# Sixteen modulation units spread anew over the recurrence's tail, a down projection and attention

## The chip, the cores and the metric

The kernel runs on one NeuronCore of a Trainium2 chip. The core has a matrix engine (TensorE, PE in the profile, with its weight loads shown as PEld), a vector engine (DVE), a scalar engine (ACT), a general engine (POOL) and a queue engine (SP) that issues nearly all transfers. Each engine runs its own instructions in the order in which they stand in the program, and waits on semaphores where it needs another engine's result. The metric is the device time of one execution in microseconds (us); lower is better.

## The reference, cut to what matters

One inference step of a two-layer encoder: a layer of RWKV-7 time mixing, then one of chunk-band attention, each followed by a gated feed-forward layer. There are 1024 prompt tokens and 8 x 16 sample tokens of width 1024, so nine conditioning vectors `c`. The vectors enter through an adaptive norm in front of each sub-layer:

```python
mod = silu(c) @ w_ada[l] + b_ada[l]                 # per layer, 1024 -> 6 * 1024
sh_m, sc_m, gt_m, sh_f, sc_f, gt_f = split(mod, 6)
x = x + gt_m * mixer(rms_norm(x) * (1 + sc_m) + sh_m)
h = rms_norm(x) * (1 + sc_f) + sh_f
x = x + gt_f * ((silu(h @ w_gate[l]) * (h @ w_up[l])) @ w_down[l])
# between the layers, for the keys and values that attention shares:
shift, scale = split(silu(c) @ kv_ada_w + kv_ada_b, 2)
k, v = split((rms_norm(x) * (1 + scale) + shift) @ w_kv, 2)
```

Everything is float32. The modulation depends on `c` alone, so it can be computed at any time before it is used.

## The kernel before

All 14 x 1024 columns of modulation (six of each layer, two of the shared keys and values) are cut into 28 **units** of 512 columns. Unit `u` fills the four columns `4u` to `4u+3` of the tile `mod`, each of 128 features by nine vectors. Units 0 to 11 belong to the first layer. Of the second, units 12 to 15 are the shift and scale in front of attention, 16 and 17 its gate, and 18 to 23 the shift, scale and gate of the feed-forward layer. Units 24 to 27 are the shift and scale of the shared keys and values.

A unit is made by `ada_steps` (line 194), a generator that other loops advance with `self.step(n)` (line 189). It has four steps. Each loads 512 KB of weights (line 201) into a tile from `rawtile` (line 226) and multiplies them with `scT` (line 204), four matmuls that the compiler issues as eight instructions, into one PSUM bank. The fourth step also copies the bank to SBUF on ScalarE (line 208), sums and turns it by four more matmuls (line 210, again eight instructions), and adds the bias on VectorE into `mod` (line 214). Consumers rescale `mod` in `gain` (line 217) and read it in `normed`, `normed_split` and `residual`.

The kernel runs through these stages:

- **Projections and recurrence** (`layer0a`, line 1088). Tokens are cut into three blocks of 384. The projections of a block are woven by hand with the recurrence's windows of the block before (`alternate`, line 1004). Units 0 to 3 run at the start. `proj` (line 461) then makes a generator of units 4 to 11, of which the last block's `proj_v` takes eight steps. The **tail** (lines 1101 to 1113) holds the last six windows, in steps, woven five to two with `early` (line 1105). This takes the remaining steps of the units, then the output projection (`outproj`, line 1062) of the first two token blocks, eight weight units each. The third block follows after the windows (line 1115). In the tail `rawtile` has two buffers, which the units, their copies and the output projection's weights share.
- **The first feed-forward layer** (`ffn`, line 1267): gate and up projections in a form with seven products instead of eight, then the **down projection** (lines 1277 to 1327). It has eleven rounds `p` of two weight rows, each with two column ranges `c`; `begin(p)` (line 1282) loads a round and calls `self.step(7)`. Units 12 to 27 run here, with PSUM bank `acc` and tiles `h0`.
- **Shared keys and values, first queries** (`kv`, line 1428).
- **Attention** (`attention`, line 1496): eight head pairs (`pair`, line 1602), sixteen query tiles each. `advance` (line 1633) starts a new tile, moves the two tiles before it one stage on (scores, softmax, transpose, output) and takes two pieces from `self.qgen`, which projects the queries of a later pair in the PSUM bank `acc` (one buffer, `head_steps`, line 1402). `kprep` and `qprep` (lines 1479, 1489) load the next pair's keys and queries. Loads here come from `slot(1)` (line 1152), a ring `h1` of fourteen tiles that also holds the normalised inputs of the sample-side columns.
- **Output projection and the second feed-forward layer.**

What stands in the code is not the final order of an engine's instructions. A planner in the compiler takes the instructions by priority (their order in the code) as a model of the machine makes them ready, and gives out buffers as they come free. A step that waits for a buffer lets a later one pass on the matrix engine, if that one is ready.

Of the kernel before, what the change touches and what calls it, by code (L numbers as in the profile page):

```python
# [10 lines left out]
AF = mybir.ActivationFunctionType  # L11
ALU = mybir.AluOpType
# [52 lines left out]
PAR = {n: i * 8 for i, n in enumerate(PARS)}  # L65
# [71 lines left out]
def mm(nc, out, lhsT, rhs, start, stop):  # L137
    return nc.tensor.matmul(out, lhsT, rhs, start=start, stop=stop)  # L138


class Trunk:
# [52 lines left out]
    def ada_steps(self, units, tag="aux", bufs=1):  # L194

        nc = self.nc
        for u in units:
            ps = self.bank(tag, bufs)
            for i in range(4):
                w = self.rawtile()  # L200
                nc.sync.dma_start(w[:, :1024], self.a["wada"][u, i])
                c = slice(i // 2 * 256, i // 2 * 256 + 256)
                for q in range(4):
                    mm(nc, ps[32 * q:32 * q + 32, c], self.scT[:, i % 2 * 4 + q, :], w[:, q * 256:q * 256 + 256], i % 2 == 0, i % 2 == 1)
                if i < 3:
                    yield
            sb = self.rawtile()[:, :512]
            nc.scalar.activation(sb, ps, AF.Copy)
            for j in range(4):
                mm(nc, ps[:, j * 16:(j + 1) * 16], sb[:, j * 128:(j + 1) * 128], self.C("qs"), True, True)  # L210
            pv = ps[:, 0:64].rearrange("p (j n) -> p j n", n=16)[:, :, 0:9]
            bo = PAR["bada"] + u * 4
            bv = self.par[:, bo:bo + 4].rearrange("p (j o) -> p j o", o=1).broadcast_to([128, 4, 9])
            nc.vector.tensor_tensor(self.mod[:, u * 4:u * 4 + 4, :], pv, bv, ALU.add)
            yield

    def gain(self, name, sc):

# [242 lines left out]
    def proj(self, b):  # L461

        if b == 0:
            self.ada = self.ada_steps((0, 2, 1, 3), "acc", 2)
            self.A0 = [self.cp.tile([128, 9], F32, name=f"A0_{f}") for f in range(8)]
            self.proj_h(0)
            self.lora_weights()
            self.x = self.hsplit()
            self.ada = self.ada_steps(range(4, 12))
        x, k = self.x, self.mixed(2, b)  # L470
        yield from self.proj_lora(b, *x)
        r = self.mixed(0, b)
        yield from self.proj_k(b, *k)
        v = self.mixed(3, b)
        yield from self.alternate(self.inverses(b), self.proj_r(b, *r))
        if b + 1 < NB:
            self.proj_h(b + 1)
        yield from self.proj_v(b, *v)
        if b + 1 < NB:
            self.x = self.hsplit()  # L480
# [607 lines left out]
    def layer0a(self, ctx):  # L1088
        self.yg = [self.dp.tile([128, 8, TB], F32, name=f"yg{b}") for b in range(NB)]
        c1, cw, ct = ExitStack(), ExitStack(), ExitStack()  # L1090
        self.ps = c1.enter_context(self.tc.tile_pool(name="psA", bufs=1, space=PSUM, reuse_waits="tile"))
        self.win_open(cw)
        with ExitStack() as c2:
            self.proj_open(c2)
            for _ in self.proj(0):
                pass
            for b in range(1, NB):
                w = self.windows([(w, hf) for w in range(3 * b - 3, 3 * b) for hf in range(2)])
                for _ in self.alternate(w, self.proj(b), 5, 4):
                    pass  # L1100
        self.tail_open(ct)
        self.nraw, self.nhi, self.nlo = (2, 2, 2)
        self.nmix, self.nmr = 16, 2

        def early():
            for _ in range(32):
                if next(self.ada, StopIteration) is StopIteration:
                    break
                yield
            for b in range(2):  # L1110
                yield from self.outproj(b)
        for _ in self.alternate(self.windows([divmod(int(x), 2) for x in '12 13 16 14 15 17'.split()]), early(), 5, 2):
            pass
        cw.close()
        for _ in self.outproj(2):
            pass
        ct.push(c1)
        return ct.close
# [148 lines left out]
    def ffn(self, l, B, W, part1, xsrc, dst, done):  # L1267

        nc = self.nc
        sd = [self.dp.tile([128, 2, 1152], F32, name=f"sd{l}_{p}") for p in range(11)]  # L1270
        self.gate_up(sd[0][:, 0], B, iter(W), (0,))
        for _ in part1:
            pass
        self.gate_up(sd[0][:, 0], B, iter(W), (1,))
        for f in range(1, 22):
            self.gate_up(sd[f // 2][:, f % 2], B, self.strassen_weights(l, f), (0, 1))
        self.ada = self.ada_steps(range(12, 28), "acc", 1) if l == 0 else iter(())
        gate = 48 * l + 40
        acc, end = {}, iter(())
        act, W = {}, {}  # L1280

        def begin(p):
            for c in range(2):
                w = (512, 640)[c]
                raw, hi, lo = (self.slot(c, dt)[:, :2 * w].rearrange("p (i t) -> p i t", i=2) for dt in (F32, F32R, F32R))
                nc.sync.dma_start(raw, sd[p][:, :, self.cols(c)])
                self.split(hi, lo, raw)
                act[p, c] = hi, lo
            W[p] = [self.halves(self.a[f"wd{l}"][f]) for f in (2 * p, 2 * p + 1)]
            self.step(7)  # L1290

        for p, c in [(p, c) for p in range(9) for c in range(2)] + [(9, 1), (10, 1), (9, 0), (10, 0)]:
                if (p, c) not in act:
                    begin(p)
                if p == 0:
                    acc[c] = self.feats(c)
                if p == 10:
                    st = self.sq_open()
                for n in range(8):
                    ns = slice(n % 4 * 128, (n % 4 + 1) * 128)  # L1300
                    d, parts = self.pz(c)
                    for z, o, m in parts:
                        for i in range(2):
                            wh, wl = W[p][i][n // 4]
                            hi, lo = (act[p, c][h][:, i, o:o + m] for h in range(2))
                            self.mm3(z, wh[:, ns], wl[:, ns], hi, lo, i == 0, i == 1)
                    y = acc[c][n]
                    if p == 0:
                        nc.scalar.activation(y, d, AF.Copy)
                    elif p <= 7:  # L1310
                        nc.vector.tensor_tensor(y, y, d, ALU.add)  # L1311
                    else:
                        self.residual(512, n, gate, y, y, d)
                    if p == 10:
                        nc.sync.dma_start(dst[:, n, self.cols(c)], y)
                        if l == 0:
                            self.sq_add(st, y, n < 6)
                    if p == 7:
                        x = self.ev("xin")[:, :y.shape[-1]]
                        nc.sync.dma_start(x, xsrc[:, n, self.cols(c)])  # L1320
                        self.residual(512, n, gate, y, x, y)
                    next(end, None)
                if p == 10:
                    for _ in end:
                        pass
                    end = done(c, acc[c], st)
        return end
# [168 lines left out]
    def attention(self, ctx):  # L1496
        nc, tc = self.nc, self.tc
# [11 lines left out]
        nc.scalar.activation(self.m1r, m1, AF.Copy)  # L1509
        self.X, self.xs = {}, {}  # L1510
        self.O = self.bank("O", 1)
        self.flow = [None] * 3
        for n in range(8):
            if n < 6:
# [87 lines left out]
    def pair(self, n):  # L1602
        nc = self.nc
# [15 lines left out]
        for i, (e, qt) in enumerate(order):  # L1619
            self.advance(self.tile(n, qt, e, vf, bias[e]))  # L1620
            if n == 6 and i in (4, 5, 6, 8, 9, 10):
                self.xprep(*divmod((4, 5, 6, 8, 9, 10).index(i), 3))
                if i == (4, 5, 6, 8, 9, 10)[2]:
                    self.qgen = self.proj_part()
            if n == 7 and i in (4, 5):
                self.xprep(i - 4, 3)
            if (e, qt) == (0, 7) and n < 7:
                self.kprep(n + 1, 1)
                self.qprep(n + 1, 1)
            if i in (1, 9):  # L1630
                self.advance(next(groups))

# [226 lines left out]
```

## Time and profile before

| what | us |
|---|---|
| timed runs: median of 3 (lowest, highest) | 3941.44 (3936.35, 3944.1) |
| the profiled execution | 3918.74 |
| its span, on which all positions below are | 3917.0 |
| PE busy | 3584.4 |
| DVE busy | 2282.2 |
| ACT busy | 1586.7 |
| first to last load of a unit's weights in the tail and just ahead of it | 917.5 to 1152.4 |
| first to last load of a unit's weights in the down projection | 1886.9 to 2164.4 |

The positions are microseconds from the span's start. The windows view gives, for a stretch of the span, the busy time of each engine with its count of instructions, the clock that the matrix engine was granted (1.00 is full speed), and the busy share and rate of the transfers. Groups by line give how many instructions of a shape there were, their busy time together and the mean of one in ns; matmuls overlap one another, so the busy time is less than count times mean. The chain of waits follows the work that ended last from piece to piece. An instruction of the matrix engine is shown by the tiles that it writes and reads: `S` and `PT` are PSUM banks of the wide products, `acc` and `aux` single banks, `st`, `G` and `Y` those of the recurrence; `raw`, `h`, `w`, `wh` are SBUF tiles. All matmuls stand on line 138, the helper that issues them.

### The profile page before, as it was taken

The page shows a single profiled execution, that of the slowest core. Times are in us where ns is not written, and L with a number is a line of the kernel's source. Part 1 is how long each engine was busy: PE and PEld are TensorE (multiplying, and loading weights), DVE is VectorE, ACT ScalarE, POOL GpSimd, SP SyncE. Part 2 cuts the span into 40 slices and gives each one's busy share as a digit, 9 for nine tenths or more (in the row PEclk, how much of TensorE's full clock was granted, in tenths as well). Part 3 has the DMA queues.
Part 4 walks back from the last instruction along what each step waited for, and adds up shares of the span by engine and source line. Part 5 has one row for each costly group of instructions (what it writes and reads, how often), then busy time and mean ns, then how long its engine had stood idle before and what let it go on. Part 6 is the DMA issues. An engine that isn't in the chain of part 4 may idle for free.

```text
span 3917.0 us, 72405 instructions
## 1 busy us (share of the span) xinstructions
PE 3584.4 (92%) x28662; PEld 3134.8 (80%) x28662; DVE 2282.2 (58%) x4355; ACT 1586.7 (41%) x2991; POOL 575.1 (15%) x473
## 2 busy tenths in 40 slices
PE   5888999889799789999999999898889899999999
PEld 3677778677568679999888878777777789999998
DVE  3567576664535765545456852566676765455567
ACT  3555556554213443333321253455654533333310
POOL 0000000000000244545100000000000165454000
PEclk9788889799679889999999999999999999999999
DMA  5775676577646422222655213355464422222522
GB/s 201 213 240 136 195 218 183 163 228 197 182 130 189 150 92 76 74 74 73 231 204 186 103 55 101 97 152 153 148 199 156 146 72 74 76 71 94 171 80 73
DMA packets 430211, 554.27 MB, mean 142 GB/s; under 512 B 128528, under 2 KB 297872, under 8 KB 425392
## 3 DMA queue, kind: packets, MB, share of 16 engines
q1 hardware_dynamic: 375728, 530.77, 42.9%
q10 hardware_dynamic: 54144, 18.89, 2.1%
q8 instruction: 225, 3.69, 0.4%
q14 instruction: 114, 0.93, 0.1%
HBM read 415.39 MB, written 134.12 MB: 140 GB/s over the span
## 4 chain that ended last, share of the span: by engine, by line
PE 63%; DMA 8%; DVE 6%; ACT 3%; issue 2%; SPq 1%; POOL 0%; ACTq 0%; DVEq 0%; POOLq 0%
PE S L138 31%; PE PT L138 15%; PE acc L138 8%; PE st L138 3%; PE O L138 2%; DVE h L254 1%; PE PT L1685 1%; PE Y L138 1%; PE G L138 1%; PE aux L138 1%; DMA mr<-yg 1%; ACT pts L1686 1%; DMA h<-qT 0%; DMA L<-ld 0%; DMA ld<-Aab 0%
## 5 line engine op out<-in xcount | busy, mean ns | idle before, releaser
L138 PE MATMUL S<-h,w 128*128 128x320 f32 (+1 forms) x4944 | 697.5, 299 | 19.4 <-DVE h L254 8.3
L138 PEld LDWEIGHTS S<-h,w 128*128 128x128 f32 x4944 | 672.9, 191 | 31.3 <-DVE h L254 15.3
L138 PE MATMUL acc<-mx,whi 128*128 128x384 f32 (+1 forms) x1824 | 529.4, 367 | 58.3 <-ACT whi L253 19.2
L138 PE MATMUL S<-h,wh 128*128 128x320 f32 (+1 forms) x2844 | 527.8, 337 | 11.8 <-DVE h L1055 6.7
L138 PEld LDWEIGHTS S<-h,wh 128*128 128x128 f32 x2844 | 454.0, 188 | 67.7 <-issue 13.3
L138 PEld LDWEIGHTS acc<-mx,whi 128*128 128x128 f32 (+1 forms) x1824 | 345.5, 197 | 93.2 <-ACT whi L253 21.0
L253 ACT ACTIVATE w<-rq 128x512 fp32r<-128x512 f32 x308 | 192.6, 629 | 515.7 <-PE S L138 205.4
L254 DVE TENSOR_TENSOR w<-rq,w 128x512 fp32r<-128x512 f32 x308 | 269.9, 880 | 195.3 <-ACT w L253 194.4
L138 PE MATMUL PT<-h,w 128*128 128x320 f32 (+1 forms) x2448 | 354.9, 300 | 9.9 <-ACT w L253 4.3
L138 PEld LDWEIGHTS PT<-h,w 128*128 128x128 f32 x2448 | 337.5, 192 | 13.8 <-DVE h L254 5.1
L138 PE MATMUL acc<-mx,wlo 128*128 128x384 f32 (+1 forms) x912 | 329.1, 361 | 2.9 <-DVE wlo L254 2.8
L138 PE MATMUL PT<-h,wh 128*128 128x320 f32 (+1 forms) x1428 | 287.0, 344 | 11.5 <-DVE wh L254 3.9
L1244 POOL TENSOR_TENSOR t<-t,t 128x576 f32<-128x576 f32 (+1 forms) x132 | 216.1, 1638 | 416.8 <-ACT t L1251 296.3
L138 PEld LDWEIGHTS PT<-h,wh 128*128 128x128 f32 x1428 | 233.5, 190 | 41.8 <-issue 6.1
L254 DVE TENSOR_TENSOR wlo<-raw,whi 128x1024 fp32r<-128x1024 f32 (+1 forms) x123 | 145.4, 1182 | 114.4 <-ACT whi L253 113.6
L138 PEld LDWEIGHTS acc<-mx,wlo 128*128 128x128 f32 (+1 forms) x912 | 179.3, 197 | 14.7 <-DVE wlo L254 5.2
L253 ACT ACTIVATE whi<-raw 128x1024 fp32r<-128x1024 f32 (+1 forms) x123 | 125.7, 1023 | 113.1 <-PE acc L138 81.5
L254 DVE TENSOR_TENSOR h<-h,h 128x1024 fp32r<-128x1024 f32 (+4 forms) x112 | 123.4, 1116 | 80.9 <-ACT h L253 66.2
L253 ACT ACTIVATE wh<-rq 128x512 fp32r<-128x512 f32 x124 | 74.7, 625 | 229.6 <-PE S L138 144.0
L253 ACT ACTIVATE h<-h 128x1024 fp32r<-128x1024 f32 (+4 forms) x112 | 103.2, 934 | 158.4 <-DMA h<-sd 94.3
L1244 DVE TENSOR_TENSOR t<-S,t 128x576 f32<-128x576 f32 (+1 forms) x116 | 86.5, 745 | 131.6 <-PE S L138 131.5
L1311 DVE TENSOR_TENSOR h<-h,S 128x640 f32<-128x640 f32 (+1 forms) x150 | 111.9, 751 | 79.6 <-PE S L138 79.3
(399 smaller groups left out, 5706.8 us busy)
## 6 DMA issues: line engine op xcount, KB each, us to landing
h<-in_wada SPq DMA_DIRECT2D x64, 512.0 KB, 6.3
raw<-in_wada SPq DMA_DIRECT2D x48, 512.0 KB, 4.4
rq<-in_wg SPq DMA_DIRECT2D x88, 256.0 KB, 2.6
rq<-in_wu SPq DMA_DIRECT2D x88, 256.0 KB, 2.6
rq<-in_wd SPq DMA_DIRECT2D x88, 256.0 KB, 3.0
kc<-in_ck SPq DMA_DIRECT2D x16, 1024.0 KB, 5.1
vc<-in_cv SPq DMA_DIRECT2D x16, 1024.0 KB, 5.8
sd<-t SPq DMA_DIRECT2D x88, 160.0 KB, 1.9
```

What stands on the lines that cost most here:

```text
L138: return nc.tensor.matmul(out, lhsT, rhs, start=start, stop=stop)
L253: self.nc.scalar.activation(hi, x, AF.Copy)
L254: self.nc.vector.tensor_tensor(lo, x, hi, ALU.subtract)
L1244: eng.tensor_tensor(out, x, y, ALU.add)
L1311: nc.vector.tensor_tensor(y, y, d, ALU.add)
L1685: nc.tensor.transpose(pt[:, j * 128:(j + 1) * 128], P[:, j * 128:(j + 1) * 128], self.C("ident"))
L1686: nc.scalar.activation(pts[:, 0:nk * 128], pt[:, 0:nk * 128], AF.Copy)
```

## The change

Of the sixteen units that ran in the first down projection, four (24 to 27) are appended to the generator that the recurrence's tail drains, and the bound on steps in `early` is raised from 32 to 64. Four (12 to 15) stay in the down projection, at two steps per round instead of seven. Eight (16 to 23) go into attention: a new generator `ada_ahead` takes two steps per unit, one that issues the four loads, into four tiles of `slot(1)`, and one that does all matmuls, the copy and the sum, in the bank `acc`. `pair` advances it behind tiles 2, 6, 10 and 14, so that two units run in each of the first four pairs. The body of `ada_steps` is cut into `ada_sum` and `ada_end`, which both generators call.

```diff
@@ ada_steps
                 nc.sync.dma_start(w[:, :1024], self.a["wada"][u, i])
-                c = slice(i // 2 * 256, i // 2 * 256 + 256)
-                for q in range(4):
-                    mm(nc, ps[32 * q:32 * q + 32, c], self.scT[:, i % 2 * 4 + q, :], w[:, q * 256:q * 256 + 256], i % 2 == 0, i % 2 == 1)
+                self.ada_sum(ps, w, i)
                 if i < 3:
                     yield
-            sb = self.rawtile()[:, :512]
...
+            self.ada_end(u, ps, self.rawtile()[:, :512])
             yield
+
+    def ada_ahead(self, units):
+
+        for u in units:
+            w = [self.slot(1)[:, :1024] for _ in range(4)]
+            for i in range(4):
+                self.nc.sync.dma_start(w[i], self.a["wada"][u, i])
+            yield
+            ps = self.bank("acc", 1)
+            for i in range(4):
+                self.ada_sum(ps, w[i], i)
+            self.ada_end(u, ps, self.slot(1)[:, :512])
+            yield
@@ proj
-            self.ada = self.ada_steps(range(4, 12))
+            self.ada = self.ada_steps((*range(4, 12), *range(24, 28)))
@@ layer0a, early
-            for _ in range(32):
+            for _ in range(64):
@@ ffn
-        self.ada = self.ada_steps(range(12, 28), "acc", 1) if l == 0 else iter(())
+        self.ada = self.ada_steps(range(12, 16), "acc", 1) if l == 0 else iter(())
@@ ffn, begin
-            self.step(7)
+            self.step(2)
@@ attention
         self.O = self.bank("O", 1)
+        self.ada = self.ada_ahead(range(16, 24))
@@ pair
+            if i in (2, 6, 10, 14):
+                self.step(1)
             if i in (1, 9):
                 self.advance(next(groups))
```

More of the change, by code (lines that the diff above doesn't have):

```diff
@@ L201, in ada_steps, with ada_sum, ada_end @@
                 nc.sync.dma_start(w[:, :1024], self.a["wada"][u, i])
-                c = slice(i // 2 * 256, i // 2 * 256 + 256)
-                for q in range(4):
-                    mm(nc, ps[32 * q:32 * q + 32, c], self.scT[:, i % 2 * 4 + q, :], w[:, q * 256:q * 256 + 256], i % 2 == 0, i % 2 == 1)
+                self.ada_sum(ps, w, i)
                 if i < 3:
                     yield
-            sb = self.rawtile()[:, :512]
[L208 to L214, printed above, removed]
-            yield
+            self.ada_end(u, ps, self.rawtile()[:, :512])
+            yield
+    def ada_ahead(self, units):
[9 more added lines that the diff above has]
+            yield
+    def ada_sum(self, ps, w, i):
+        c = slice(i // 2 * 256, i // 2 * 256 + 256)
+        for q in range(4):
+            mm(self.nc, ps[32 * q:32 * q + 32, c], self.scT[:, i % 2 * 4 + q, :], w[:, q * 256:q * 256 + 256], i % 2 == 0, i % 2 == 1)
+    def ada_end(self, u, ps, sb):
+        nc = self.nc
+        nc.scalar.activation(sb, ps, AF.Copy)
+        for j in range(4):
+            mm(nc, ps[:, j * 16:(j + 1) * 16], sb[:, j * 128:(j + 1) * 128], self.C("qs"), True, True)
+        pv = ps[:, 0:64].rearrange("p (j n) -> p j n", n=16)[:, :, 0:9]
+        bo = PAR["bada"] + u * 4
+        bv = self.par[:, bo:bo + 4].rearrange("p (j o) -> p j o", o=1).broadcast_to([128, 4, 9])
+        nc.vector.tensor_tensor(self.mod[:, u * 4:u * 4 + 4, :], pv, bv, ALU.add)
     def gain(self, name, sc):
```

## The prediction

> **What bounds the kernel now.** I read the page's slices first: PE, the matrix engine, is busy nearly everywhere, so a unit that is moved is worth the difference between the PE time that it takes at its old place and at its new one. The windows view shows the places (the two feed-forward down projections, then the recurrence's tail in two parts, the stretch behind it, the middle of attention):
>
> ```profile
> core 0: us, PE busy (x) PEld busy (x) DVE busy (x) ACT busy (x) POOL busy (x), PEclk, DMA share, GB/s
> 1903.84:2218.82 314.98, 314.98 (x2129) 262.37 (x2129) 184.12 (x303) 68.24 (x96) 6.94 (x5) 1.00 0.54 191
> 3634.77:3891.25 256.48, 255.63 (x1490) 235.12 (x1489) 177.69 (x281) 54.28 (x73) 0.00 (x0) 1.00 0.33 105
> 1010.00:1178.00 168.00, 147.42 (x1701) 104.28 (x1702) 69.09 (x183) 33.61 (x71) 0.00 (x0) 0.65 0.56 162
> 1178.00:1312.00 134.00, 132.53 (x1158) 108.81 (x1158) 72.37 (x136) 49.61 (x84) 0.00 (x0) 0.95 0.59 180
> 1312.00:1430.00 118.00, 79.39 (x333) 65.31 (x331) 87.17 (x166) 57.42 (x116) 46.37 (x39) 0.76 0.36 120
> 2560.00:2800.00 240.00, 217.20 (x1905) 178.19 (x1897) 158.54 (x481) 142.21 (x332) 1.30 (x9) 0.96 0.47 143
> ```
>
> The first two rows run from the first PE instruction of a down projection to the start of its last sixteen groups. In the first layer (with the units) PE is busy for all of 314.98 us at the full clock; in the second (without) the same work takes 256.48 us. So PE bounds this stage, with no gap in which a unit could hide. In the tail's first part, where six units run now, PE is busy 147 of 168 us, but at a granted clock of 0.65. In its second part, where the output projection fills in, it is busy 132.5 of 134 at 0.95. Behind the tail, and in attention, PE has gaps: 38.6 of 118 us and 22.8 of 240.
>
> **Down projection: twelve units out.** The sixteen units now there cost 314.98 - 256.48 = 58.5 us, or 3.66 us each. The groups by line agree:
>
> ```profile
> L138 PE MATMUL acc<-h,scT 128*32 128x256 f32 x512 | 40.6, 387 | 0.0
> L138 PE MATMUL acc<-cst,h 128*128 128x16 f32 x128 | 15.7, 249 | 0.0
> ```
>
> (40.6 + 15.7) / 16 = 3.5 us of a unit's own matmuls; the rest is lost where the stream of large matmuls is cut. Twelve units out: 12 x 3.66 = **-43.9 us**. Nothing is late in their place: the second layer ran the stage without them at 255.63 busy of 256.48 us. Their 48 loads and 12 copies on ScalarE go too, worth nothing here, since PE never waited for them (0.0 in both rows). I hold this term to within 4 us. That the last four units come earlier costs nothing at the shared K/V, which only reads them.
>
> **The tail: four units in.** Sixteen steps (a 512 KB load and eight matmul instructions each) follow the 24 that run there now; the range of 64 lets them all run before the output projection's first unit, and both use the two `raw` buffers. Today's order shows it: the first output weight is loaded when the last step is through.
>
> ```profile
> L138 PE MATMUL aux<-raw,scT x192: 376/605/637, 1013.3 to 1174.1; 128*32 128x256 f32 x192
> L138 PE MATMUL aux<-raw,scT x56: 376/391/637, 1096.8 to 1118.2; 128*32 128x256 f32 x56
> L246 SPq DMA_DIRECT2D raw<-in_rw_o x20: 328/333/530, 1174.6 to 1306.7; - x20
> SPq L201 <- PE aux L138: 47.7, 15, 11.5
> ```
>
> The first row is 192 / 8 = 24 steps in 168 us, 7.0 us per step; the second, the densest 32 us (1094 to 1126), is 7 steps, 4.6 us per step. The last row says that SP, the queue of nearly all loads, stood 47.7 us behind a step whose buffer was not free; the recurrence's own loads, output stores and loads of `yg` stand behind such a wait too. So the added steps delay the output projection, which now fills the gaps of the last windows, by 16 x 4.6 = 74 us or by 16 x 7.0 = 112 us. I take 74: the late windows have no more triangular inverses to merge, as in the dense stretch. It would start at 1175 + 74 = 1249.
>
> What is left for PE then? From 1178 to 1312 it did 132.53 x 0.95 = 126 us of full-clock work. One piece of the chain prices the output matmuls:
>
> ```profile
> 1208.83 4.23 PE acc L138 x23
> ```
>
> 4.23 / 23 = 0.184 us; 16 units x 24 = 384 of them are 70.5 us, and one unit of the third block (4.4 us) falls in there, so the windows took some 51 us. In 74 us, busy at 93% and a clock of 0.8 (between the 0.65 and 0.95 above), PE does 55 us of full-clock work: the four units (4 x 3.66 = 14.6) and 40 us of windows. There remain 11 + 70.5 = 81.5 us, at 0.95 some 86: the two blocks end near 1335, 23 us later than now. The lower bound is a tail that stays dense, 14.6 / 0.95 = 15 us. The upper is 7.0 us per step: start at 1287, windows all but done (112 x 0.88 x 0.65 = 64 us of work), then 72 us: 1360, 48 later.
>
> Part of this comes back, since the last window no longer ends last:
>
> ```profile
> 1313.83 1.11 PE st L138 x2
> ...
> 1318.96 2.28 DMA yg<-y
> 1321.25 0.02 SPq L1070
> 1321.27 0.03 issue
> 1321.30 2.47 DMA mr<-yg
> ...
> 1325.78 6.58 DMA x<-x
> ```
>
> Here PE waits from the last window's normalisation to the third block's inputs, some 12 us. With the windows through by 1300 that wait is covered by output matmuls. Against more, the stretch to 1430 holds 87.17 us of DVE work, most of which needs the blocks' results. I take 12 back (0 to 20): **+11 us** net, bounds -5 and +48.
>
> [...]
>
> **Attention: eight units in.** Two in each of the first four head pairs. Their matmuls cost 8 x 3.66 = 29.3 us at the full clock, 30.5 at 0.96. The existing filler, the query projections, already runs there at two pieces per tile, and PE keeps gaps of 22.8 us in 240, short ones behind ScalarE's evictions. One longer wait comes at each turn to the next pair:
>
> ```profile
> 2650.19 5.20 DMA h<-qT
> 2714.85 4.93 DMA h<-qT
> L1493 SPq DMA_DIRECT2D h<-qT x12: 450/457/584, 2532.9 to 2834.4; - x12
> ```
>
> If all the gaps took filler the cost would be 30.5 - 22.8 = 8 us. None taken, it is 30.5, and something is added: a unit takes four of the fourteen `h1` slots at once. By the code eight hold the normalised inputs and three the keys and queries, so three are left, and the loads of `kT`, `qT` and the query weights use the same ones. A unit's slots are free only when its matmuls have run, and these need the single `acc` bank, which a query projection holds for eight pieces. The second unit of a pair is loaded at tile 10 and used at tile 14, just where the next pair's keys are loaded. If each of four turns waits one load more (5 us by the rows above), 20 us are added: 50. SP is in order, so stores of `o` and loads of the cache stand behind a load without a slot. Copies on ScalarE (eight of 0.6 us) and the DVE sums beside them lie on engines with room (142 and 159 of 240). I take **+24 us**: a quarter of the matmuls hidden, no more, since the gaps are short and in program order PE cannot choose what fills them.
>
> **The sum.** -43.9 + 11 + 24 = -9 us. The profiled execution took 3918.74 us (span 3917.0), below all three timed runs (3936 to 3944, median 3941.44); the difference is set against the median: **3932 us**. A measurement of this kernel tells about 0.2%, 8 us, from no change.
>
> **Rivals.**
> - *The tail gives it back* (slower). If the added steps run at the 7.0 us of today's first part, the windows crawl at 0.65 with them and all sixteen output units come afterwards: -43.9 + 48 - 10 + 24 = +18, 3959 us. It decides from about 6 us per step. For it: the 47.7 us of SP's wait, and 24 steps that took 168 us. Against: the dense 32 us at 4.6. Chance 0.22.
> - *Attention's turns wait* (no change or slower). The slots bring 46 to 50 us: -43.9 + 11 + 46 = +13, 3954 us. For it: the loads of `qT` stand on the chain of waits at each turn. Against: the planner can run a unit's matmuls early. Chance 0.18.
> - *The gaps take it all* (faster). [...] For it: 22.8 and 38.6 us of gaps. Against: filler is there already. Chance 0.20.
> - *It does not do what it says*: the planner orders by readiness, and the added steps could sink into the output projection, or the attention's into later pairs, with a time near no change. The step counts (40 in the tail, 16 by step(2) in eight rounds, 16 in four pairs) finish before each use, so 0.05.
> - The forecast itself: 0.35, spread from -25 to 0 by its terms.
>
> **How the numbers follow.** Faster by over 0.2%: 0.22 of the forecast's 0.35 and 0.20 of the gaps' case, 0.42. Same: 0.13 of the forecast, 0.05 of attention's, 0.02 of the tail's, 0.05: 0.25. Slower: 0.20 and 0.13: 0.33. Low end: -43.9 - 5 + 8 = -41, 3901. Both upper bounds together would be -43.9 + 48 + 50 = +54; leaving out that corner, the range reaches to +29, 3970. The forecast's own range is 3916 to 3941.
>
> **What would show it.** In the changed kernel the first layer's down projection should take some 271 us between the same two marks (256.5 + 4 x 3.66); were it over 280, the first term is wrong. The first load of an output weight should come near 1250 and the two blocks end near 1335; a start past 1275 with a clock near 0.65 is the first rival. The first four pairs should each be 6 us longer, without longer waits for `qT` at their turns; 10 us or more is the second rival, 2 the third. The gate and up projections and the whole second feed-forward layer should keep their lengths.

## The result and the profile after

| what | us |
|---|---|
| before, six timed runs: median (lowest, highest) | 3935.65 (3922.32, 3944.1) |
| after, six timed runs | 3965.76 (3957.55, 3977.1) |
| after against before | 1.0086, interval 1.0069 to 1.0104 |
| profiled execution after; its span | 3977.1; 3975.3 |

The change makes the kernel slower, by 0.86% or some 34 us. Forecast was 3932, 9 us faster; the time lies inside the range, on the other side of zero.

The profiled execution of after is the slowest of its six runs and that of before is below all of its own, so the two spans lie 58 us apart and not 34. I therefore compare stage by stage and take the verdicts from the ratios. The first table gives marks from the groups by line, in us from the start of the span: the first unit step (eight of the 32 steps run just ahead of the tail; the first of their loads is at 880.4 us in before, not at 917.5 as in the table of before), the first and last load of an output weight, the first unit matmul of the down projection (its start), and the first and last load of `vf`, the values of a head pair. The first `vf` is issued ahead of pair 0, the last at the end of pair 5: 720 of the 960 matmuls that read `vf` lie between the two, so this stretch holds six pairs. The expectations below call it the first eight pairs.

| mark | before | after | difference from the mark above, after less before |
|---|---|---|---|
| first unit step | 914.2 | 927.3 | +13.1 |
| first output weight | 1174.6 | 1287.0 | +99.3 |
| last output weight | 1363.9 | 1411.7 | -64.6 |
| start of the down projection | 1903.8 | 1963.9 | +12.3 |
| first `vf` | 2529.2 | 2546.9 | -42.4 |
| last `vf` | 2907.6 | 2964.3 | +39.0 |
| end of the span | 3917.0 | 3975.3 | +1.6 |

The 13.1 us lie in code that the change does not touch; over the executions shown below this mark falls anywhere from 910.5 to 926.6. From the first unit step to the down projection after takes 47 us more (99.3 - 64.6 + 12.3), the down projection and the shared keys and values 42 less, six pairs of attention 39 more.

The windows view of after, with the columns of the prediction's first fence: the down projection between the two marks of the prediction, the tail from where units 24 to 27 begin to the first output weight, the stretch of the output projection, and the stretch behind it.

```profile
1963.87:2238.63 274.76, 274.31 (x1650) 242.60 (x1650) 180.21 (x287) 61.45 (x84) 6.94 (x5) 1.00 0.40 131
1191.00:1287.00 96.00, 84.05 (x922) 53.39 (x921) 26.16 (x70) 18.07 (x36) 0.00 (x0) 0.70 0.47 141
1287.00:1412.00 125.00, 108.57 (x538) 93.55 (x539) 76.69 (x134) 54.61 (x89) 1.90 (x1) 0.96 0.69 216
1412.00:1490.00 78.00, 51.56 (x237) 43.30 (x236) 62.76 (x116) 37.70 (x78) 43.45 (x38) 0.77 0.27 87
```

The first row is the gain: 274.76 against 314.98 us. The second holds four units and what windows ran beside them: 96 us at a clock of 0.70, where before, with output matmuls in that place, had 0.95. The output projection then fills 1287 to 1412 well, but its last weight comes later, and PE idles for a third of the 78 us behind it (26.4 us; in the 78 us behind the last output weight of before it is 15.6).

The groups by line of after give the tail's start (they answer to the prediction's `raw` rows), and its waits from 911 us on what held it:

```profile
L138 PE MATMUL aux<-raw,scT x384: 379/460/637, 927.3 to 1286.3; 128*32 128x256 f32 x192
L266 SPq DMA_DIRECT2D raw<-in_rw_o x24: 327/332/1123, 1287.0 to 1411.7; - x24
```

```profile
SPq L201 <- PE aux L138: 94.0, 30, 11.5
PE aux L138 <- DMA raw<-in_wada: 19.5, 12, 4.0
```

SP waited 94.0 us for a `raw` tile whose reader on PE had not run, and PE waited 19.5 us for loads of units. Only 10.1 us of that, in six waits, lie in the 96 us of the added steps; for most of these PE is busy (84.05 us), at a clock of 0.70. The timeline of after shows two such waits; the bracket is the idle time before a piece and what ended it:

```profile
1234.66 1.08 PE L138 MATMUL aux<-raw,scT 128*32 128x256 f32 x8
1238.04 1.08 PE L138 MATMUL aux<-raw,scT 128*32 128x256 f32 x8 [2.30 <-DMA raw<-in_wada]
1240.86 1.08 PE L138 MATMUL aux<-raw,scT 128*32 128x256 f32 x8 [0.69 <-DMA raw<-in_wada]
```

The eight matmuls of a step take 1.08 us; the steps come about 3 us apart here. With two tiles a load takes the tile of the step two before it: SP issues the next one at 1235.80, 0.06 us behind the end of the first step's matmuls, and the third step's start 5.06 us later. Over the sixteen added steps the mean is 6.2 us (99.3 / 16).

In attention, the windows view from the first to the last `vf` and of the pair in which after loses most, with the group that loads query weights, of before and then of after (pair 4 holds no unit: the last matmul of one is at 2826):

```profile
2529.20:2907.60 378.40, 330.57 (x2888) 268.46 (x2889) 251.75 (x756) 221.04 (x511) 2.32 (x16) 0.94 0.53 161
...
2796.00:2848.00 52.00, 44.44 (x424) 35.02 (x421) 37.68 (x115) 32.09 (x71) 0.29 (x2) 0.97 0.59 170
```

```profile
L235 SPq DMA_DIRECT2D h<-in_wq x12: 327/346/530, 2524.4 to 2825.0; - x12
```

```profile
2546.90:2964.30 417.40, 362.54 (x3208) 283.51 (x3209) 251.31 (x766) 224.55 (x519) 2.33 (x16) 0.94 0.60 187
...
2829.00:2903.00 74.00, 61.43 (x520) 49.53 (x519) 45.08 (x138) 41.28 (x98) 0.29 (x2) 0.90 0.55 157
```

```profile
L255 SPq DMA_DIRECT2D h<-in_wq x12: 328/342/432, 2542.7 to 2876.3; - x12
```

PE is busy 32 us longer and idle 7 us longer. The last load of query weights comes 329 us behind the first `vf` and not 296, and pair 4 issues 96 PE instructions more (520 against 424) without a unit: the units pushed query work back into a pair that had been short. By pairs 0 to 5, before took 71, 59, 64, 59, 52 and 59 us, after 69, 71, 66, 62, 74 and 61.

### The profile page after: what moved, and what is told of

Its sections match the earlier page's. It is cut to its first block, busy times and chain, and to the rows that moved or that the text cites. A ratio compares the mean times of both kernels' runs of the same rounds, so it can differ in the third digit from the quotient of the medians.

```text
span 3975.3 us, 72455 instructions
## 1 busy us (share of the span) xinstructions
PE 3617.1 (91%) x28662; PEld 3161.2 (80%) x28662; DVE 2275.7 (57%) x4355; ACT 1587.4 (40%) x2991; POOL 574.7 (14%) x473
## 4 chain that ended last, share of the span: by engine, by line
PE 61%; DMA 8%; DVE 7%; ACT 3%; issue 2%; SPq 1%; POOL 0%; ACTq 0%; DVEq 0%; POOLq 0%
PE S L138 30%; PE PT L138 15%; PE acc L138 7%; PE st L138 3%; PE O L138 2%; DVE h L274 1%; PE PT L1708 1%; PE aux L138 1%; PE G L138 1%; PE Y L138 1%; DMA mr<-yg 1%; DMA raw<-in_wada 1%; DMA h<-out_kT 1%; DMA h<-qT 1%; DMA ld<-Aab 0%
## 5 line engine op out<-in xcount | busy, mean ns | idle before, releaser
L138 PEld LDWEIGHTS PT<-h,w 128*128 128x128 f32 x2448 | 337.3, 192 | 14.8 <-DVE h L274 4.9
L138 PE MATMUL acc<-h,wh 128*128 128x256 f32 (+1 forms) x864 | 134.7, 305 | 11.6 <-ACT wh L273 8.6
```

## The experiments

Each ratio is against the kernel before on the same chip in the same session. E1 and E2 split the change; E3, E4, E6, E7, E8 and E12 ask why the tail costs so much, E5, E9, E10, E11 and E13 the same of attention.

**E1, the tail alone.** Units 24 to 27 in the tail, all others in the down projection:

```diff
-        self.ada = self.ada_steps(range(12, 16), "acc", 1) if l == 0 else iter(())
+        self.ada = self.ada_steps(range(12, 24), "acc", 1) if l == 0 else iter(())
-            self.step(2)
+            self.step(7)
-        self.ada = self.ada_ahead(range(16, 24))
+        self.ada = iter(())
```

> The tail's part of the change alone: units 24 to 27 join the recurrence's tail, the twelve others stay in the down projection (seven steps a round), attention holds none. Delay theory (the sixteen steps keep the two raw buffers, so the output projection starts about 110 us later and no longer fills the windows' gaps): the tail grows by 47 us, the down projection shrinks by 4 x 3.66 = 15 us, in all +32 us, ratio 1.008, first output weight loaded near 1290. Rival (a unit costs its own matmul time, 3.7 us at full clock and some 5.5 us at a clock of 0.65): +0 to +8 us, 1.000 to 1.002.

Measured 3952.08 us, ratio 1.0061 (1.0048 to 1.0073). The four units alone make most of the loss, nearer to the delay theory than to its rival, though the first output weight comes at 1274.3 and the stretch grows by 37 us, not 47; that does not show yet that the delay is the cause.

**E2, attention alone.** Units 24 to 27 go back into the down projection.

```diff
-            self.ada = self.ada_steps((*range(4, 12), *range(24, 28)))
+            self.ada = self.ada_steps(range(4, 12))
-        self.ada = self.ada_steps(range(12, 16), "acc", 1) if l == 0 else iter(())
+        self.ada = self.ada_steps((*range(12, 16), *range(24, 28)), "acc", 1) if l == 0 else iter(())
-            self.step(2)
+            self.step(7)
```

> Attention's part alone: units 16 to 23 in attention, units 12 to 15 and 24 to 27 in the down projection, the tail as before. Additive theory (all of the matmul time of the eight units, 30 us, lands on the path, and some 9 us of waits beside it): attention +39, down projection -29, in all +10 us, ratio 1.0025. The forecast's theory (a quarter hidden): -5 us, 0.999. Gaps theory: -21 us, 0.995.

Measured 3938.83 us, 1.0028 (1.0015 to 1.0040). 0.61% and 0.28% make 0.89% against the change's 0.86%: two costs that add, as the additive theory has it.

**E3, the units behind the output projection of the first two blocks**, so that its start is not delayed (on top of E1's edits, as in E4 and E6):

```diff
-            for _ in range(64):
-                if next(self.ada, StopIteration) is StopIteration:
-                    break
+            for _ in range(24):
+                next(self.ada, None)
                 yield
             for b in range(2):
                 yield from self.outproj(b)
+            for _ in range(16):
+                next(self.ada, None)
+                yield
```

> As the tail alone, but the sixteen added steps stand behind the output projection of the first two token blocks instead of ahead of it; the same units in the same stage, only their order differs. Delay theory: the first output weight is loaded near 1175 again and nearly all of the 47 us goes: the tail costs 0 to 15 us, in all -15 to 0 us, ratio 0.996 to 1.000. Rival (the units' own time): no better than the tail alone.

**E4, the units in the third block's output projection**, two steps behind each of its weight units (the first change as in E3, without the second loop):

```diff
         for _ in self.outproj(2):
-            pass
+            self.step(2)
+        self.step(16)
```

> As the tail alone, but the sixteen added steps are taken two at a time between the eight weight units of the third block's output projection, where PE has gaps (38.6 us of the 118 us behind the tail). If gaps there can take them: tail stage +0 to +8, in all -15 to -7 us, ratio 0.996 to 0.998. If the steps lengthen that chain by their matmul time at the low clock there (0.76): +19 - 15 = +4 us, 1.001.

Measured: E3 3951.53 us, 1.0062 (1.0043 to 1.0081); E4 3951.31 us, 1.0062 (1.0045 to 1.0078). Both expectations fell, the delay theory's first; the rival of E3 (no better than the tail alone) has the right number. By the groups by line, output weights are loaded from 1175.6 to 1397.8 us in E3 and from 1178.4 to 1406.7 in E4. The output projection now starts as in before (1174.6), yet its last weight comes 34 and 43 us later than 1363.9. Four units cost the same at three places, so the cause is hardly the late start of the output projection, and rather what the units are made of. The waits of SP's queue in E4 between 1178 and 1440 us point to it:

```profile
SPq L201 <- DVE wlo L274: 26.3, 8, 10.4
SPq L266 <- PE aux L138: 26.1, 7, 6.6
```

A unit's load waits until a weight's second half is split off, and a weight's load until a unit's matmuls have run: both in the two `raw` tiles. That gave a new theory, the round trip through this ring, with two tests: take the loads away, or add a tile.

**E6, no loads for units 24 to 27**; their matmuls read constants.

```diff
+                if u < 24:
                     w = self.rawtile()
                     nc.sync.dma_start(w[:, :1024], self.a["wada"][u, i])
                     self.ada_sum(ps, w, i)
+                else:
+                    self.ada_sum(ps, None, i)
```

> The run with four units in the tail alone, but these four units load no weights: their matmuls read constants, so 16 loads and 16 uses of the ring of two raw tiles are gone, while all their matmuls, copies and steps stay. It leaves out the right modulation of units 24 to 27. Theory (loads into a ring of two tiles): the matmuls alone take 4 x 4 to 5.6 us in the tail against the 11 to 15 us that leave the down projection, so the ratio falls from 1.006 to 1.000 to 1.0025, and the tail's stage is 10 to 22 us longer than before, not 37. Rival (TensorE's own time at the low clock, and the chain of matmul, copy, matmul): the ratio stays at 1.005 to 1.007.

**E7, E1 with three raw tiles; E8, the kernel before with three; E12, the whole change with three.** One line in each:

```diff
-        self.nraw, self.nhi, self.nlo = (2, 2, 2)
+        self.nraw, self.nhi, self.nlo = (3, 2, 2)
```

> Four units in the tail alone, with three raw tiles in the tail in place of two. Theory (loads into a ring of two): a third tile lets the next load start a step earlier; the ratio falls from 1.006 to 1.000 to 1.003, and the waits of SP's queue for the units' matmuls (92.7 us with two tiles) fall by half. Rival (TensorE's own time, or one unit's chain): 1.005 to 1.007.

> The kernel before, with three raw tiles in the tail in place of two: the control for the run above. Theory (ring of two): before's own eight units in the tail, and the weights of the third block, gain too; 0.994 to 0.999. Rival: nothing there waits for raw tiles in the end; 0.999 to 1.001.

> The whole change with three raw tiles in the tail in place of two. Theory (two separate costs): the tail's part falls as it did with the four units alone, from 1.0061 to 0.9990, the attention's stays, so the ratio falls from 1.0086 to 1.000 to 1.003, and the stretch from the tail's first step to the down projection's first unit is 5 to 17 us longer than before, not 47. Rival (what is saved in the tail is waited for later): 1.005 or more.

| run | ratio (interval) | first, last output weight | first unit step to down projection |
|---|---|---|---|
| before | 1 | 1174.6, 1363.9 | 989.6 |
| E1, two tiles | 1.0061 (1.0048 to 1.0073) | 1274.3, 1396.3 | 1026.7 |
| E3, units last | 1.0062 (1.0043 to 1.0081) | 1175.6, 1397.8 | 1025.3 |
| E4, third block | 1.0062 (1.0045 to 1.0078) | 1178.4, 1406.7 | 1028.5 |
| E6, no loads | 0.9985 (0.9971 to 0.9999) | 1201.5, 1364.5 | 996.9 |
| E7, three tiles | 0.9990 (0.9976 to 1.0004) | 1224.2, 1372.7 | 1000.5 |
| E8, before, three tiles | 0.9965 (0.9953 to 0.9977) | 1126.5, 1348.3 | 981.3 |
| the change, two tiles | 1.0086 (1.0069 to 1.0104) | 1287.0, 1411.7 | 1036.6 |
| E12, the change, three tiles | 1.0030 (1.0017 to 1.0043) | 1209.4, 1364.3 | 1006.4 |

The last column scatters by itself: executions of E2, E5, E9, E10, E11 and E13, whose tail is that of before, show 989.4 to 1003.6. The ratios therefore carry the verdict, and they agree: without loads the same matmuls cost less than the down projection gives back (0.76% less than E1, and below the theory's own range), and one more tile saves 0.71% in E1 (also just below the range), 0.56% in the change and 0.35% even in before. E12 came out at the upper edge of what the theory allowed. The groups by line of E6 and, below, of E7 and E8, show how:

```profile
L138 PE MATMUL aux<-cst,scT x128: 379/379/635, 1185.8 to 1205.1; 128*32 128x256 f32 x128
```

```profile
L138 PE MATMUL aux<-raw,scT x384: 376/403/637, 926.6 to 1224.9; 128*32 128x256 f32 x192
```

```profile
L138 PE MATMUL aux<-raw,scT x256: 379/414/637, 910.5 to 1125.9; 128*32 128x256 f32 x128
```

Without loads all sixteen steps pass in 19 us. With loads, the first output weight comes 260.4 us behind the first unit step in before and 352.4 in E1, so the sixteen added steps take 92.0 us, 5.8 each. With a third tile it is 216.0 in E8 and 297.6 in E7: the added steps still take 81.6 us, 5.1 each, and of the 55 us that the tile gains in E7, 44 lie in steps that before has too. SP's waits for the units' matmuls fall from 92.7 us in E1 (30 waits) to 56.5 in E7 (21), by less than the half that was expected.

E7 stays 0.25% above E8, so four units in the tail still cost more than in the down projection, with three tiles too; the whole change with three tiles stays 0.65% above E8. The loads are shown as the cost (E6), the ring of two as a part of it: of the 0.61% of the move, some 0.36 goes with the third tile when before has it as well. The rest of what a load does is not taken apart. SP's first 851 transfers, to 1170 us in before, come in the same order in before and after, while the lag between the two varies by 22.7 us among them; so the recurrence's own transfers stand behind a unit's load that waits for its tile (92.7 us in E1). No run issues the tail's loads from another queue. The transfer engines are not full there: their share is 0.47 in the stretch of the added steps, 0.69 in the next. E8 is faster than both kernels of this case: 3912.42 us, against 3927.92 for the kernel before beside it.

**E5, attention's matmuls without loads and the four slots for them (the slot of the copy stays); E10, slots without loads; E9, loads from POOL.** From E2:

```diff
@@ E5
-            w = [self.slot(1)[:, :1024] for _ in range(4)]
-            for i in range(4):
-                self.nc.sync.dma_start(w[i], self.a["wada"][u, i])
...
-                self.ada_sum(ps, w[i], i)
+                self.ada_sum(ps, None, i)
@@ E10
-                self.nc.sync.dma_start(w[i], self.a["wada"][u, i])
+                self.nc.gpsimd.memset(w[i], 0.0)
@@ E9
-                self.nc.sync.dma_start(w[i], self.a["wada"][u, i])
+                self.nc.gpsimd.dma_start(w[i], self.a["wada"][u, i])
```

In E5 and E6 `ada_sum` takes columns of the constants where it is given no tile.

> Eight units in attention at the same places as in the run with attention alone, but without their 32 loads and the 32 slots for them: the matmuls read constants in their place. It leaves out the right modulation of units 16 to 23. Theory (matmul time): the units' matmuls cost what they cost in the down projection and more, whatever brings their weights, so the ratio stays where that run was, 1.002 to 1.0035, and the first eight pairs stay some 35 to 43 us longer. Rival (loads and slots): the loads and the slots push the queries' and keys' work back and make the long fifth pair; without them the pairs grow by 25 us or less and the ratio is 0.9985 to 1.0005.

> Eight units in attention alone, with their slots taken as in the run of that kind, but each slot is filled with zeros by POOL in place of a load. It leaves out the right modulation of units 16 to 23. Theory (SP's order, or the transfers): no load of the units in SP's queue and no transfer, so the pairs are 15 to 25 us longer and the ratio is 0.998 to 1.0005. Rival (the slots: fewer of the fourteen are left for keys and queries): the pairs stay 33 us longer or more and the ratio at 1.002 to 1.0035.

> Eight units in attention alone, as before in the run of that kind, but their 32 loads are issued by POOL, which is busy 2 us in the whole stretch, and not by SP. The slots and the matmuls stay. Theory (SP's order): in SP's queue a load that waits for a slot holds up the loads and stores of keys, queries and values behind it; on POOL it holds up nothing, so the first eight pairs fall from 43 us longer to 15 to 25 (18 was measured without loads and slots) and the ratio from 1.0028 to 0.998 to 1.0005. Rival (the slots themselves, or the transfers' share of the DMA engines): the pairs stay 33 us longer or more, ratio 1.002 to 1.0035.

**E11, the slots from the other ring of fourteen; E13, units in halves**, two slots at a time and one unit a pair. From E2:

```diff
@@ E11
-            w = [self.slot(1)[:, :1024] for _ in range(4)]
+            w = [self.slot(0)[:, :1024] for _ in range(4)]
...
-            self.ada_end(u, ps, self.slot(1)[:, :512])
+            self.ada_end(u, ps, self.slot(0)[:, :512])
@@ E13
-            w = [self.slot(1)[:, :1024] for _ in range(4)]
-            for i in range(4):
-                self.nc.sync.dma_start(w[i], self.a["wada"][u, i])
-            yield
+            for h in range(2):
+                w = [self.slot(1)[:, :1024] for _ in range(2)]
+                for i in range(2):
+                    nc.sync.dma_start(w[i], self.a["wada"][u, 2 * h + i])
+                yield
...
```

> Eight units in attention alone, loads on SP, but the five slots of a unit come from the other ring (that of the left columns, h0) and not from the ring through which the raw keys, queries and query weights pass. Theory (slots of that ring): the first eight pairs fall from 43 us longer to 15 to 30, ratio 0.998 to 1.001. Rival (the transfers, or SP's order): still 33 us longer or more, 1.002 to 1.0035.

> Eight units in attention alone, each done in two halves: two slots, two loads, then eight matmuls and the end for two of its four blocks of rows; one unit a pair over all eight pairs. The same loads and almost the same matmuls. Theory (slots held at a time): half the slots are held, the first eight pairs are 20 to 32 us longer, ratio 0.9985 to 1.0015. Rival (transfers, or matmul time): 35 us or more, 1.002 to 1.004.

The windows view from the first to the last `vf`, in this order: E2, E5, E10, E9, E11, E13.

```profile
2512.70:2934.10 421.40, 364.80 (x3208) 286.29 (x3209) 251.55 (x766) 224.98 (x519) 2.35 (x16) 0.93 0.59 185
```

```profile
2508.20:2905.00 396.80, 350.03 (x3208) 280.19 (x3209) 252.78 (x766) 225.62 (x519) 2.46 (x16) 0.95 0.50 154
```

```profile
2516.10:2924.40 408.30, 360.81 (x3208) 282.97 (x3209) 257.00 (x766) 226.28 (x519) 32.85 (x48) 0.95 0.49 150
```

```profile
2502.50:2925.40 422.90, 365.12 (x3208) 287.05 (x3209) 251.43 (x766) 224.51 (x519) 19.45 (x48) 0.93 0.59 185
```

```profile
2511.40:2978.30 466.90, 380.84 (x3208) 298.35 (x3209) 255.52 (x766) 229.54 (x519) 2.39 (x16) 0.88 0.52 167
```

```profile
2509.10:2902.20 393.10, 343.48 (x3111) 272.75 (x3111) 248.91 (x761) 221.47 (x518) 2.80 (x16) 0.96 0.59 184
```

| run | longer than before's 378.4 us | ratio (interval) |
|---|---|---|
| E2, four slots and loads | 43.0 | 1.0028 (1.0015 to 1.0040) |
| E5, matmuls alone | 18.4 | 0.9983 (0.9970 to 0.9996) |
| E10, slots, no loads | 29.9 | 1.0020 (1.0006 to 1.0034) |
| E9, loads from POOL | 44.5 | 1.0053 (1.0034 to 1.0071) |
| E11, the other ring | 88.5 | 1.0174 (1.0152 to 1.0196) |
| E13, two slots at a time | 14.7 | 1.0008 (0.9994 to 1.0022) |

E5 contradicts the theory of matmul time: the same 3208 matmul records in the stretch, but 0.45% less time. Of E2's 24.6 us over E5, 14.8 are PE busy longer with the same instructions, at a clock of 0.93 and not 0.95, and 9.8 are idle. Moving the loads out of SP's order gains nothing (E9: 1.0053 against 1.0028). There the wait only moves to POOL's queue, which stands idle 177.7 us ahead of the 32 loads, the largest part of it until PE matmuls into `acc`, which read such tiles, are through:

```profile
L213 POOL DMA_DIRECT2D h<-in_wada x32 | 17.1, 533 | 177.7 <-PE acc L138 65.7 <-DVE st L1702 28.6 <-DVE wh L274 16.4
```

Slots without any transfer (E10) bring back 0.37% of the 0.45%. In us it is 11.5 of 24.6, between the ranges of theory and rival, so a part for the transfers stays possible; the intervals of E10 and E2 overlap, and I can't tell it from zero by ratio. E10's fills are work of their own, too: POOL is busy 32.85 us, and DVE 257.00 us on its 766 instructions against 251.55 in E2, so the share of the slots alone may be smaller. Half the slots at a time takes 0.20% off E2, with intervals that overlap; its 14.7 us leave out the last units, which run behind the last `vf` (to 3012 us). Two things change in E13 at once, the slots held and the spread over eight pairs, so it supports the slots and does not show them alone. E11 met neither theory nor rival: its stretch has 86 us of PE idle (466.9 - 380.8) against 48 in before. By the code, the other ring holds two of three tiles of keys and queries, for whole pairs. It was the wrong ring to take from, and says only that its slots cost far more, 88.5 us against 43.0.

## Why the prediction went wrong, point by point

- **Down projection (-43.9): right.** 314.98 - 274.76 = 40.2 us between its own marks, 3.35 us per unit where 3.66 were taken; 274.8 against the 271 named as the sign.
- **The tail (+11 net): the failed step.** I took 4.6 us per step from the densest 32 us, for the reason that late windows have no triangular inverses to merge. The sixteen steps took 6.2 each (99.3 us of delay), and the output projection began at 1287.0, where the upper bound of 7.0 us per step had put it (13.1 us of that lie ahead of the first step). The stage became 47 us longer, close to the bound of +48 (whose last 72 us of output matmuls I had not divided by the 0.95; with that it is +51), and by E1 the move of four units costs 0.61%. The first rival had said that it decides from about 6 us per step, and its signs came (start past 1275, clock 0.70); its own price for the stage, 48 - 10 = +38, was too low by 9. But its mechanism, windows that crawl while the output units come afterwards, is not what costs: E3 gave the output projection its old start and lost the same. What costs is the units' loads, which I had counted only through the pace of the steps: I priced what a unit adds to PE, and without its loads the sixteen steps take 19 us (E6), near the lower bound of 15, and the loss is gone. The ring of two `raw` tiles is a shown part of that (some 0.36 of the 0.61%). I had quoted its row, 47.7 us of SP waiting for PE, and took no price from it; whether it costs through the steps or through the transfers that stand behind them in SP's queue, no run separates.
- **The 12 us taken back** came in part and were lost again: between the first and the last output weight PE's idle time fell from 24.7 to 16.4 us, and in the 78 us behind the last one it rose from 15.6 to 26.4.
- **Attention (+24): its matmuls were near, its chosen value was not.** The matmuls alone cost 18.4 us (E5), less than my 24. The slots and loads, which I had worked out only for the upper bound (three free of fourteen, 20 us), were real: 39.0 us in the change, 43.0 in E2. The second rival had the cause and nearly the price (46), but not the place: of the first four pairs only pair 1 grew by 10 us or more (12), and pair 0 not at all. The largest single growth, 22 us, stands in pair 4 behind the last unit, where query projections that came late were done.
- **The sum.** By stages -42 + 47 + 39 = +44 us, where the upper bounds together had been +54: the corner that I left out of the range as unlikely. The ratio's 34 us are the firmer figure, as the stages come from one execution of each kernel. It was not two accidents. In both terms I priced what the units add to PE, and in both their loads and the tiles that they hold cost more than that. That the time still lies inside the stated range is luck: the range reached to +29 us and the loss by ratio is 34, but before came out at 3935.65 and not at the 3941.44 against which the range was set.
- **The clock (0.8 taken).** In the stretch of the added steps it was 0.70, with PE busy for 84.05 of 96 us, where the stretch with output matmuls had 0.95 in before.

Of the ring's part the trace shows twelve waits of PE for a unit's load (19.5 us from 911 us on), and the runs 0.9990 with a third tile against 1.0061.

**Open:** the share of the transfers themselves in attention; whether E9 is really slower than E2 (the intervals overlap, and its stretch is 1.5 us longer); and how the loads turn into lost time in the tail, since three tiles leave four units there dearer than in the down projection (0.25% between E7 and E8) and PE itself waits only 10.1 us for them in the 96 us of the added steps.

## What to carry to other kernels

Work that is moved into gaps is priced by all that it holds, not by its matmuls (in attention 18.4 us for these alone, 43.0 with slots and loads): count the tiles that it takes from each ring and the time from claim to release. Where a queue's waits already name a buffer, more work through it can cost far more than its matmuls, as in the tail (1.0061 with the loads, 0.9985 without); try one more buffer before moving the work, since here that gained 0.35% and the move lost 0.86%. And if two terms of a sum rest on the same cheap assumption, their upper bounds belong in the range together.

## What was not expected of the hardware

Four units cost the same 0.61 to 0.62% at three different places, two in the tail and one in the third block behind it. And stretches with identical code differ between executions: the tail of before, in seven kernels that share it, took 989.4 to 1003.6 us. A loss below some 14 us can't be read from one pair of profiles of this kernel, only from repeated times.
